# RWKV-7 head pairs in two merged instruction streams, dense products dealt out by a virtual clock

## The chip, the cores and the metric

One core of one Trainium2 chip runs the whole program. The metric is the device time of one execution in microseconds (us), the median of repeated runs; lower is better.

## The reference

Two layers, 512 tokens of width 1024, float32. Each layer adds half a SwiGLU feed-forward block, then a mixer of three branches, then a second half block. What matters here is the mixer, and in it the RWKV-7 branch with eight heads of 64:

```python
h = rms_norm(x, norm_mix[l])
proj = h @ w_in                                  # retention, sparse attention, rwkv and gate columns
y_ret, y_dsa = retention(...), sparse_attention(...)
# rwkv: token shift, low-rank decay and rate, normalised key kk, then for each token
def step(S, inp):
    r_t, w_t, k_t, v_t, kk_t, a_t = inp
    sa = jnp.einsum('bhvk,bhk->bhv', S, -kk_t)
    S = S * w_t[:, :, None, :] + sa[..., None] * (kk_t * a_t)[:, :, None, :] + v_t[..., None] * k_t[:, :, None, :]
    return S, jnp.einsum('bhvk,bhk->bhv', S, r_t)
# group norm of y over each head, + bonus, * g
merged = g_ret * (y_ret @ p_ret) + g_dsa * (y_dsa @ p_dsa) + g_rwkv * (y_rwkv @ p_rwkv)
x = x + merged @ w_out
```

## The kernel before

**Dense products.** Each float32 operand is split in a high and a low part (`split`, lines 49 and 50: ACT copies, DVE subtracts), and a product of 128x128 by 128x512 is three one-pass matmuls (`mm3`, lines 109, 111 and 113) into a PSUM bank with the tag psd (four banks). "A product" below is one of these three matmuls. Weights come through SP's queue into four raw buffers and three split ones.

**RWKV.** The eight heads are worked in four pairs. A pair has these steps, named as in the prediction:
- the front (`front2`): decay (lines 346-360, `cum`, `E`), rate, normalised key (line 373, the Newton steps `kkr` of `rsqrt`, `bc` in line 378 and its transposes by line 96), bonus (392, 393), and the stacked operands `bk` and `stk` (403 to 406), partly on DVE and partly on POOL;
- the mixing products z (line 421, four groups), with their two masked evacuations on DVE (426, 427);
- the inverse (in `mid`): the 32x32 diagonal blocks go through DRAM (`dn`) into N, one block a partition; POOL solves the triangular systems in 31 steps (466, 468); after every fourth a one-column "pace" matmul (470) stands in PE's order; the result goes through DRAM (`dx`) into `mt`, and two rounds of small matmuls (487, 492) join the blocks;
- the chain (`chain`): eight chunks of 64 tokens one after the other, each with four hops: A (line 504), copied to `cx`; B (514), copied to `uv`; C (524), which with `cb` gives the next state `sv`; and D (531), whose result goes to `Y`;
- the post (`post`): group norm of Y, transposes, bonus, gate (564), and y to DRAM.

The recurrence has two PSUM banks of its own (tag psr); retention and attention use two others (psf).

**Order.** A tile scheduler takes instructions by priority levels; `K.at("rec")` puts the recurrence in the first level. The other dense products of the mixer (retention, attention, gates, merge) are queued, and `K.fill(n, after=mm)` places n of them behind the matmul `mm`. How many stand behind which step was written in tables by hand: 11 behind each z group, 38 behind v's transposes, 12, 11, 11 or 15 behind each pace, 29 behind the last pace, 5 behind each join, 9, 7, 3 or 5 behind each hop of the chain, 46 behind the chain, and 6, 0, 2 or 7 that stand behind no step. Pairs follow one another: chain(p), the front, z and inverse of p + 1, then post(p). Retention and the index part of the attention run beside pairs 0 and 1, the attention's heads beside pairs 2 and 3, and the merge, which needs all three branches, comes last.

## Time and profile before

| what | value |
|---|---|
| median of 3 runs | 3111.48 us (3107.99 to 3112.62) |
| span of the profiled execution, first to last instruction | 3103.6 us |
| PE busy | 2990.3 us (96%) |
| DVE, ACT, POOL busy | 1761.8, 1081.5, 715.2 us |
| mean granted clock of PE | 0.975 |
| core, state | one core, clock as granted by the throttle |

The execution's own time is its span and some 8 us around it, by the median of the runs. PE is busy nearly throughout; matmuls are pipelined, so a busy PE is not PE at its peak, and at a granted clock of 0.5 the same work is busy twice as long. What an idle or slow stretch costs is read from windows of the span.

### The profile page before, as it was taken

To read this page: it belongs to the slowest core of one execution; us is meant where nothing else is said; L and a number is where in the kernel's file an instruction comes from. 1 tells how busy PE (TensorE), PEld (TensorE's weight loads), DVE (VectorE), ACT (ScalarE), POOL (GpSimd) and SP (SyncE) were. 2 spreads that over 40 slices of the span, in tenths; PEclk is the share of its full clock that TensorE was granted. 3 is DMA by queue.
4 is the path that set the end of the run, shared out by engine and by line. 5 is a ranking of instruction groups with operands and counts; after the bars stand their busy time and mean duration, and the time that the engine had idled before them with its cause. 6 is when DMAs were issued, how large, how long until landed. Compare 5 with 4: busy or idle time off the path is not lost.

```text
span 3103.6 us, 40717 instructions
## 1 busy us (share of the span) xinstructions
PE 2990.3 (96%) x14336; PEld 2373.5 (76%) x14336; DVE 1761.8 (57%) x3641; ACT 1081.5 (35%) x1892; POOL 715.2 (23%) x1186
## 2 busy tenths in 40 slices
PE   9999999999899999999999999999999899999998
PEld 7888877767667778888888888677776677788886
DVE  5443388758675675443344433887585746644433
ACT  4333343334333233333333333433333333333322
POOL 2110024342433031111011101243423340311100
PEclk9999999999899999999999999899999999999999
DMA  4223422223223452233322234222333135523232
GB/s 136 98 97 106 117 72 70 73 85 124 81 85 96 139 190 95 95 99 94 97 95 97 98 109 118 66 72 71 96 110 92 64 110 155 175 92 99 96 95 89
DMA packets 203580, 314.08 MB, mean 101 GB/s; under 512 B 46320, under 2 KB 60400, under 8 KB 203376
## 3 DMA queue, kind: packets, MB, share of 16 engines
q1 hardware_dynamic: 203376, 311.49, 32.2%
q8 instruction: 112, 1.84, 0.2%
q14 instruction: 92, 0.75, 0.1%
HBM read 277.86 MB, written 33.55 MB: 100 GB/s over the span
## 4 chain that ended last, share of the span: by engine, by line
PE 74%; DVE 10%; POOL 6%; DMA 6%; issue 3%; ACT 1%; SPq 0%; DVEq 0%; POOLq 0%; ACTq 0%
PE psd L113 22%; PE psd L109 22%; PE psd L111 22%; DMA N<-dn 3%; POOL cum L468 2%; POOL E L466 2%; DVE wlo L50 2%; PE psr L421 1%; DMA th<-th 1%; PE psr L504 1%; PE psf L96 1%; DMA dx<-cum 1%; DMA y<-y 1%; DVE cb L523 1%; PE psr L514 1%
## 5 line engine op out<-in xcount | busy, mean ns | idle before, releaser
L49 ACT ACTIVATE whi<-raw 128x512 fp32r<-128x512 f32 (+2 forms) x920 | 571.5, 622 | 1259.6 <-PE psd L111 927.2
L50 DVE TENSOR_TENSOR wlo<-raw,whi 128x512 fp32r<-128x512 f32 (+2 forms) x920 | 657.6, 715 | 560.0 <-ACT whi L49 543.9
L111 PE MATMUL psd<-xl,whi 128*128 128x512 f32 x2144 | 856.0, 399 | 2.4 <-DVE xl L161 2.4
L109 PE MATMUL psd<-xh,whi 128*128 128x512 f32 x2144 | 850.6, 397 | 1.5 <-DVE g L203 1.5
L113 PE MATMUL psd<-xh,wlo 128*128 128x512 f32 x2144 | 849.9, 396 | 0.1
L111 PEld LDWEIGHTS psd<-xl,whi 128*128 128x128 f32 x2144 | 406.7, 190 | 88.9 <-DVE xl L161 4.4
L109 PEld LDWEIGHTS psd<-xh,whi 128*128 128x128 f32 x2144 | 406.6, 190 | 88.5 <-issue 3.4
L113 PEld LDWEIGHTS psd<-xh,wlo 128*128 128x128 f32 x2144 | 406.9, 190 | 84.1 <-issue 1.4
L207 POOL TENSOR_TENSOR u<-s,u 128x512 f32<-128x512 f32 x88 | 141.2, 1605 | 841.0 <-DVE u L206 726.3
L109 PE MATMUL psd<-ah,whi 128*128 128x512 f32 x704 | 277.4, 394 | 0.0
L113 PE MATMUL psd<-ah,wlo 128*128 128x512 f32 x704 | 276.0, 392 | 0.0
L111 PE MATMUL psd<-al,whi 128*128 128x512 f32 x704 | 273.2, 388 | 0.0
L172 POOL TENSOR_TENSOR sq<-sq,sq 128x512 f32<-128x512 f32 x42 | 56.1, 1336 | 467.4 <-ACT sq L170 467.4
L113 PE MATMUL psd<-whi,xl 128*128 128x512 f32 (+1 forms) x384 | 160.6, 418 | 0.0
L111 PE MATMUL psd<-wlo,xh 128*128 128x512 f32 (+1 forms) x384 | 156.1, 407 | 0.0
L113 PEld LDWEIGHTS psd<-ah,wlo 128*128 128x128 f32 x704 | 132.1, 188 | 31.0
L109 PE MATMUL psd<-whi,xh 128*128 128x512 f32 (+1 forms) x384 | 155.1, 413 | 0.0
L111 PEld LDWEIGHTS psd<-al,whi 128*128 128x128 f32 x704 | 132.2, 188 | 29.6
L109 PEld LDWEIGHTS psd<-ah,whi 128*128 128x128 f32 x704 | 132.3, 188 | 26.3
L50 DVE TENSOR_TENSOR al<-u,ah 128x512 fp32r<-128x512 f32 x88 | 61.8, 702 | 153.6 <-ACT ah L49 153.4
L206 DVE TENSOR_TENSOR u<-psd,rb 128x512 f32<-128x512 f32 x88 | 60.9, 692 | 127.3 <-PE psd L113 127.3
L810 POOL TENSOR_SCALAR L<-L,mx 128x128 f32<-128x128 f32 (+3 forms) x64 | 71.4, 1118 | 199.4 <-DVE mx L809 99.0
(262 smaller groups left out, 3907.2 us busy)
## 6 DMA issues: line engine op xcount, KB each, us to landing
raw<-in_wf_dram SPq DMA_DIRECT2D x184, 256.0 KB
raw<-in_ffa_in_dram SPq DMA_DIRECT2D x176, 256.0 KB
raw<-in_ffb_in_dram SPq DMA_DIRECT2D x176, 256.0 KB
th<-th SPq DMA_DIRECT2D x96, 256.0 KB
raw<-in_ffa_out_dram SPq DMA_DIRECT2D x80, 256.0 KB
raw<-in_wt_dram SPq DMA_DIRECT2D x80, 256.0 KB
raw<-in_ffb_out_dram SPq DMA_DIRECT2D x80, 256.0 KB
x<-x SPq DMA_DIRECT2D x32, 256.0 KB
```

The costliest lines, as they stand in the source:

```text
L49: self.nc.scalar.activation(hi, x, AF.Copy)
L50: self.nc.vector.tensor_tensor(out=lo, in0=x, in1=hi.bitcast(F32), op=ALU.subtract)
L96: return self.nc.tensor.transpose(out, x, self.ident)
L109: nc.tensor.matmul(out, ah, bh, start=start, stop=False)
L111: nc.tensor.matmul(out, ah, bl, start=False, stop=False)
L113: nc.tensor.matmul(out, al, bh, start=False, stop=stop)
L172: nc.gpsimd.tensor_tensor(out=sq, in0=sq, in1=self.ssq[0], op=ALU.add)
L206: nc.vector.tensor_tensor(out=u, in0=pu, in1=self.rb, op=ALU.mult)
L207: nc.gpsimd.tensor_tensor(out=u, in0=s, in1=u, op=ALU.mult) # 2 * silu(g) * u
L466: nc.gpsimd.tensor_tensor(out=tv, in0=X[:, 0:n, u:u + 1].to_broadcast([P, n, w]), in1=N[:, u:u + 1, u + 1:].to_broadcast([P, n, w]), op=AL ...
L468: nc.gpsimd.tensor_tensor(out=X[:, 0:n, u + 1:], in0=X[:, 0:n, u + 1:], in1=tv, op=ALU.add)
L810: nc.gpsimd.tensor_scalar(out=x, in0=x, scalar1=mx[:, 3:4], scalar2=None, op0=ALU.mult)
```

## The change

The content of each engine is the same: the same matmuls, evacuations and transfers. What changes is the order, and the buffers that it needs.

- The front, z and inverse of a pair (`ahead`) and the chain and post of a pair (`behind`) become two generators that yield, after each step, a duration written by hand (in units of a microsecond: 4, 2, 4, 4, 5 for the front, 3 for each z group, 25 for the way to N, 4 for each pace, 15 for the way back, 2 for each join and each hop, 8 and 2 for the post).
- Two virtual clocks add up these durations. The stream whose clock is behind is traced next: so pair p + 1 is traced beside pair p. The chain of a pair starts when its `ahead` has ended.
- Each advance of the lower clock makes 3.2 products due for a unit; they are placed behind the last matmul traced (`self.mm`). The tables by hand go.
- `gch`, both `stk`, `zb`, `bkt`, both `sv` and `mt` get two buffers; to make room, N lies in a buffer of the tag `bk`, post uses one new tag `yq` in place of `rsq` and `bc`, two temporaries of retention and attention share other tags, and the scratch of the descriptors is set to 1024.
- The pace matmuls take a psr bank each time in place of one for all eight.

```diff
     def pairs(self, blk):
...
-        nxt = self.next(0)
-        for p in range(4):
-            d = nxt
-            K.fill(FM[p])
-            with K.at("rec"):
-                self.chain(d)
-            K.fill()
-            if p < 3:
-                nxt = self.next(p + 1)
-            with K.at("rec"):
-                self.post(d)
+        d, t, n, due = [None] * 4, [0.0, 0.0], [0, 0], 0.0
+        g = [self.ahead(d, p) for p in range(4)], [self.behind(d, p) for p in range(4)]
+        now = lambda: t[0] if n[1] == n[0] else t[1] if n[0] == 4 else min(t)
+        while n[1] < 4:
+            e = 0 if n[0] < 4 and (n[1] == n[0] or t[0] <= t[1]) else 1
+            was = now()
+            try:
+                with K.at("rec"):
+                    t[e] += next(g[e][n[e]])
+            except StopIteration:
+                n[e] += 1
+                if e == 0 and n[1] == n[0] - 1:
+                    t[1] = max(t)
+            else:
+                due += RATE * max(now() - was, 0.0)
+                if due >= 1:
+                    K.fill(int(due), self.mm)
+                    due -= int(due)
         self.done = True
...
+    def ahead(self, d, p):
+        self.K.fill()
+        d[p] = yield from self.front2(p, *self.rkv)
+        yield from self.mid(d[p])
+
+    def behind(self, d, p):
+        yield from self.chain(d[p])
+        yield from self.post(d[p])
...
-            if FI and (u % 4 == 3 or u == 30):
-                pace = nc.tensor.matmul(pz[0:1, u:u + 1], X[:, 0, u + 1:u + 2], K.ident[:, 0:1], start=True, stop=True)
-                K.fill(FI if u < 30 else FD, pace)
+            if u % 4 == 3 or u == 30:
+                self.mm = nc.tensor.matmul(K.ps("r")[0:1, 0:1], X[:, 0, u + 1:u + 2], K.ident[:, 0:1], start=True, stop=True)
+                yield 4 if u < 30 else 15
...
-            K.fill(FC[d["p"]], mm)
+            yield 2
```

In PE's program order, this is the front of pair 2 before, in the first layer, from the transposes of `bc` (line 96) to the first z group (421); names are out<-in, psr is the recurrence, psf the attention, psd the dense products:

```order
L96 MATMUL psr_7617<-ident,bc_7615 128x128 x4
L392 MATMUL psr_7626<-P_7627,bones_3109 128x512
L823 MATMUL psf_6061<-X_6067,v_3127 128x256
L393 MATMUL psr_7626<-P_7628,bones_3109 128x512
L824 MATMUL psf_6061<-X_6068,v_3127 128x256
L823 MATMUL psf_6061<-X_6067,v_3127 128x256
L824 MATMUL psf_6061<-X_6068,v_3127 128x256
L710 MATMUL psf_6082<-kh_3322,qs_5996 128x256
L711 MATMUL psf_6082<-kl_3323,qs_5996 128x256
L710 MATMUL psf_6091<-kh_3322,qs_5999 128x256
L711 MATMUL psf_6091<-kl_3323,qs_5999 128x256
L421 MATMUL psr_7648<-stk_1754_7636,bk_7638 128x128 x4
```

And this is PE's order after the change around the first z group of pair 1, in the first layer; lines have moved by 11 to 13: 515 is A, 525 B, 542 D of pair 0's chain, and 433 is pair 1's z:

```order
L515 MATMUL psr_5289<-sv_995_4238,stk_930_3960 128x64
L542 MATMUL psr_5219<-uv_1210_5251,zb_3993 64x64
L542 MATMUL psr_5219<-uv_1211_5252,zb_3993 64x64
L515 MATMUL psr_5289<-sv_996_4239,stk_931_3961 128x64
L111 MATMUL psd_5119<-wlo_5280,xh_2537 128x512
L113 MATMUL psd_5119<-whi_5279,xl_2538 128x512
L109 MATMUL psd_5120<-whi_5279,xh_2537 128x512
L433 MATMUL psr_5296<-stk_1206_5238,bk_5240 128x128 x4
L111 MATMUL psd_5120<-wlo_5280,xh_2537 128x512
L113 MATMUL psd_5120<-whi_5279,xl_2538 128x512
L109 MATMUL psd_5121<-whi_5279,xh_2537 128x512
L525 MATMUL psr_5289<-cx_5304,mt_4827 64x64 x2
```

A z group that had attention matmuls ahead of it and no dense product now stands inside a chain chunk of the pair before, with three products ahead of it and three behind.

On DVE, this is the stretch between the copies cx and uv of a chunk of pair 0's chain before (507 and 518), beside retention (601, 602, and the `rr` steps) and a split (50):

```order
L507 COPY cx_5204<-psr_5046 128x128
L601 TENSOR_TENSOR X_5053<-X_5053,rcc 128x256
L149 TENSOR_TENSOR rr_4783<-rr_4782 128x8
L602 TENSOR_TENSOR X_5053<-X_5053,m_5055 128x256
L150 SCALAR_TENSOR_TENSOR rr_4783<-rr_4783,ss_4754 128x8
L151 SCALAR_TENSOR_TENSOR rr_4782<-rr_4783,rr_4782 128x8
L50 TENSOR_TENSOR wlo_5256<-raw_5253,whi_5255 128x512
L518 COPY uv_1188_5206<-psr_5046 64x64
L518 COPY uv_1189_5207<-psr_5046 64x64
```

And the same stretch after, of the chunk shown above (518 is cx and 529 uv; 614 and 615 are retention's 601 and 602, 438 and 439 are the evacuations of pair 1's z):

```order
L518 COPY cx_5304<-psr_5289 128x128
L150 SCALAR_TENSOR_TENSOR rr_4518<-rr_4518,ss_4489 128x8
L614 TENSOR_TENSOR X_4998<-X_4998,rcc 128x256
L151 SCALAR_TENSOR_TENSOR rr_4517<-rr_4518,rr_4517 128x8
L615 TENSOR_TENSOR X_4998<-X_4998,S_5000 128x256
L149 TENSOR_TENSOR rr_4518<-rr_4517 128x8
L438 TENSOR_TENSOR zb_5295<-psr_5296,zmask 64x512
L439 TENSOR_TENSOR stk_1206_5238<-psr_5296,zmask 64x512
L150 SCALAR_TENSOR_TENSOR rr_4518<-rr_4518,ss_4489 128x8
L529 COPY uv_1220_5306<-psr_5289 64x64
L529 COPY uv_1221_5307<-psr_5289 64x64
```

Two evacuations of the other pair's z have come between the copies, where one split stood.

At the end of the first layer's RWKV work, PE's order before runs from the chain's last chunks (504 A, 514 B, 524 C, 531 D) to the first product of the merge (psd<-yh):

```order
L504 MATMUL psr_9504<-sv_1992_8819,stk_1966_8692 128x64
L531 MATMUL psr_9459<-uv_2130_9475,zb_8703 64x64
L531 MATMUL psr_9459<-uv_2131_9476,zb_8703 64x64
L504 MATMUL psr_9504<-sv_1993_8820,stk_1967_8693 128x64
L514 MATMUL psr_9504<-cx_9523,mt_9219 64x64 x2
L524 MATMUL psr_9504<-uv_2141_9525,bkt_8806 64x64
L524 MATMUL psr_9504<-uv_2142_9526,bkt_8806 64x64
L504 MATMUL psr_9560<-sv_1992_8819,stk_1966_8692 128x64
L531 MATMUL psr_9504<-uv_2141_9525,zb_8703 64x64
L531 MATMUL psr_9504<-uv_2142_9526,zb_8703 64x64
L504 MATMUL psr_9560<-sv_1993_8820,stk_1967_8693 128x64
L109 MATMUL psd_9431<-yh_2096_9383,whi_9434 128x512
```

After the change, the stretch ahead of the first product of the merge holds transposes of the attention and of Y (line 96), the attention's last matmuls (836, 837) and the gate (577); D of the last chunk stands ten rows further up, with no dense product in between:

```order
L96 MATMUL psf_6827<-ident,L_6794 128x128
L96 MATMUL psf_6827<-ident,L_6793 128x128
L96 MATMUL psf_6827<-ident,L_6794 128x128
L96 MATMUL psr_9731<-ident,Y_9158 64x128 x4
L96 MATMUL psr_9755<-ident,Y_9158 64x128 x4
L836 MATMUL psf_6813<-X_6832,v_3127 128x256
L837 MATMUL psf_6813<-X_6833,v_3127 128x256
L836 MATMUL psf_6813<-X_6832,v_3127 128x256
L837 MATMUL psf_6813<-X_6833,v_3127 128x256
L577 MATMUL psr_9770<-sg_3592,g_703_3107 128x512
L109 MATMUL psd_9614<-yh_2155_9566,whi_9617 128x512
L109 MATMUL psd_9695<-yh_2155_9566,whi_9698 128x512
```

The chain's last steps stood around the merge's first products; now the whole post stands ahead of them.

## Rows read from the trace of the kernel before

**Rows 1.** The page's busy times over the span: us, share, instructions.
```profile
PE 2990.3 (96%) x14336; PEld 2373.5 (76%) x14336; DVE 1761.8 (57%) x3641; ACT 1081.5 (35%) x1892; POOL 715.2 (23%) x1186
```

**Rows 2.** Busy time by stretches of the span, core 0: stretch, width, then busy us and instructions of PE, PE's weight loads, DVE, ACT, POOL, then PE's granted clock, the DMA share and GB/s. The second and fourth stretch of the program are the mixers; the one between them is the feed-forward block behind the first mixer and the one ahead of the second.
```profile
380.00:1170.00 790.00, 743.17 (x3842) 565.90 (x3842) 544.93 (x1291) 288.20 (x532) 261.91 (x523) 0.95 0.33 102
1170.00:1920.00 750.00, 750.00 (x3330) 620.39 (x3329) 331.45 (x524) 251.05 (x411) 91.52 (x65) 1.00 0.32 98
1920.00:2710.00 790.00, 742.03 (x3827) 564.60 (x3827) 545.04 (x1288) 287.23 (x531) 261.86 (x523) 0.95 0.33 102
```

**Rows 3.** The same columns, for the steps of the first layer's mixer: fronts with z, inverses with their transfers, pair 0's chain, and the passage to the merge.
```profile
422.00:454.00 32.00, 28.26 (x106) 20.33 (x106) 30.92 (x69) 8.45 (x17) 7.64 (x9) 0.79 0.15 46
454.00:506.00 52.00, 46.79 (x216) 34.26 (x215) 40.46 (x100) 19.23 (x33) 30.52 (x81) 0.97 0.24 72
506.00:612.00 106.00, 105.95 (x646) 80.84 (x645) 83.46 (x216) 35.47 (x61) 27.94 (x51) 1.00 0.24 76
612.00:648.00 36.00, 32.91 (x163) 25.67 (x163) 28.81 (x67) 12.02 (x22) 12.38 (x20) 0.92 0.23 70
648.00:702.00 54.00, 48.90 (x245) 36.93 (x244) 23.90 (x49) 20.30 (x38) 29.80 (x86) 0.97 0.30 90
...
766.00:812.00 46.00, 39.99 (x178) 30.36 (x178) 38.58 (x92) 15.87 (x33) 12.58 (x14) 0.85 0.24 74
812.00:864.00 52.00, 47.89 (x249) 36.29 (x248) 24.28 (x50) 21.51 (x41) 25.68 (x71) 0.97 0.33 98
...
912.00:956.00 44.00, 36.59 (x156) 26.98 (x155) 36.35 (x82) 13.58 (x26) 13.16 (x9) 0.84 0.20 62
956.00:1005.00 49.00, 45.65 (x227) 34.73 (x226) 19.42 (x38) 18.80 (x36) 25.37 (x69) 0.97 0.41 116
1018.00:1046.00 28.00, 25.37 (x140) 19.19 (x138) 16.31 (x49) 8.96 (x16) 1.51 (x6) 0.82 0.42 134
```

**Rows 4.** PE's waits over the span: what waited, for which line; us in total, times, longest.
```profile
PE psr L470 <- POOL cum L468: 25.4, 14, 4.9
PE psr L96 <- DVE bc L378: 19.7, 6, 4.4
...
PE psr L421 <- DVE bk L403: 7.8, 6, 2.7
```

**Rows 5.** The chain that ended last, pair 1 of the first layer, from the last z group to `mt`: start, us, what. The first row covers one z group (four matmuls, two records each).
```profile
640.00 1.10 PE psr L421 x8
...
642.20 1.62 DMA dn<-zb
643.91 10.71 DMA N<-dn
...
688.72 4.71 DMA dx<-cum
693.49 1.70 DMA mt<-dx
```

**Rows 6.** POOL's instructions of the inverse, over the span (eight inverses): count, busy us, mean ns, and the idle time ahead of them with what ended it.
```profile
L468 POOL TENSOR_TENSOR cum<-cum,E 128x60 f32<-128x60 f32 (+24 forms) x248 | 87.4, 353 | 16.9
L466 POOL TENSOR_TENSOR E<-cum,N 128x60 f32<-128x60 f32 (+24 forms) x248 | 80.2, 324 | 84.0 <-DMA N<-dn 59.9 <-issue 7.8
```

**Rows 7.** PE's timeline at the end of the first layer's RWKV work: start, us, instruction; in brackets the idle time ahead of it. 824 is the attention's last matmul, 514 and 524 are B and C of a chain chunk, psd<-yh the merge's first product.
```profile
1030.36 0.28 PE L824 MATMUL psf<-X,v 128*128 128x256 f32 x1
...
1033.37 0.48 PE L514 MATMUL psr<-cx,mt 64*64 64x64 f32 x4 [0.38 <-DVE cx L507]
1034.51 0.48 PE L524 MATMUL psr<-uv,bkt 128*64 128x64 f32 x4 [0.65 <-DVE uv L518]
...
1036.84 1.20 PE L109 MATMUL psd<-yh,whi 128*128 128x512 f32 x2
```

**Rows 8.** DVE's instructions by line over the span, those of the chain, of z's evacuations, of retention and of the splits: count, busy us, mean ns, idle time ahead.
```profile
L50 DVE TENSOR_TENSOR wlo<-raw,whi 128x512 fp32r<-128x512 f32 (+2 forms) x920 | 657.6, 715 | 560.0 <-ACT whi L49 543.9 <-DMA raw<-in_wf_dram 5.9 <-PE psd L113 5.3
...
L523 DVE TENSOR_SCALAR cb<-sv,gch 64x64 f32<-64x64 f32 x112 | 35.4, 316 | 2.1
L527 DVE SCALAR_TENSOR_TENSOR sv<-psr,gch,cb 64x64 f32<-64x64 f32 x112 | 31.6, 282 | 13.3 <-PE psr L524 10.7
...
L535 DVE TENSOR_TENSOR Y<-psr,cx 64x64 f32<-64x64 f32 x128 | 28.4, 222 | 9.9 <-PE psr L531 7.7
L518 DVE COPY uv<-psr 64x64 f32<-64x64 f32 x128 | 28.2, 220 | 25.5 <-PE psr L514 24.0 <-issue 0.2
...
L427 DVE TENSOR_TENSOR stk<-psr,zmask 64x512 f32<-64x512 f32 x32 | 22.0, 689 | 0.7
L426 DVE TENSOR_TENSOR zb<-psr,zmask 64x512 f32<-64x512 f32 x32 | 22.0, 687 | 9.9 <-PE psr L421 9.8
...
L601 DVE TENSOR_TENSOR X<-X,rcc 128x256 f32<-128x256 f32 x32 | 16.7, 522 | 13.5 <-POOL m L598 13.4
...
L602 DVE TENSOR_TENSOR X<-X,m 128x256 f32<-128x256 f32 x32 | 15.3, 479 | 0.2
```

**Rows 9.** DVE's second Newton operation on 128x8 elements, in the front (kkr) and in the retention (rr); the columns are those of the group above.
```profile
L150 DVE SCALAR_TENSOR_TENSOR kkr<-kkr,s 128x8 f32<-128x8 f32 x24 | 8.1, 337 | 0.5
...
L150 DVE SCALAR_TENSOR_TENSOR rr<-rr,ss 128x8 f32<-128x8 f32 x24 | 4.7, 194 | 0.3
```

More of the change, by code (lines that the diff above doesn't have):

```diff
@@ L275, in wide @@
         nc.tensor.matmul(z, self.wa[h][:, ch], self.lh[h], start=True, stop=False)
-        nc.tensor.matmul(z, self.wa[h][s, ch], self.ll[s], start=False, stop=True)
+        self.mm = nc.tensor.matmul(z, self.wa[h][s, ch], self.ll[s], start=False, stop=True)
         return z
@@ L314, in pairs @@
         K = self.K
-        K.run(self.lora(blk))
-        K.run(self.front(0, blk))
+        with K.at("norm"):
+            K.run(self.lora(blk))
+            K.run(self.front(0, blk))
         self.blk = blk
-        nxt = self.next(0)
-        for p in range(4):
-            d = nxt
-            K.fill(FM[p])
-            with K.at("rec"):
-                self.chain(d)
-            K.fill()
-            if p < 3:
-                nxt = self.next(p + 1)
-            with K.at("rec"):
-                self.post(d)
-        self.done = True
-    def next(self, p):
-        with self.K.at("rec"), ExitStack() as es:
-            if self.gate:
-                es.enter_context(self.tc.issue_after(self.gate.ins))
-            d = self.front2(p, *self.rkv)
-            self.mid(d)
-            return d
+        d, t, n, due = [None] * 4, [0.0, 0.0], [0, 0], 0.0
[16 more added lines that the diff above has]
+                    due -= int(due)
+        self.done = True
+    def ahead(self, d, p):
[5 more added lines that the diff above has]
+        yield from self.post(d[p])
     def front2(self, p, r, k, v):
@@ L372, in front2 @@
         for i in range(4):
-            nc.tensor.matmul(pss[:, 2 * i:2 * i + 2], sq[:, i * P:(i + 1) * P], c["ind2"], start=True, stop=True)
+            self.mm = nc.tensor.matmul(pss[:, 2 * i:2 * i + 2], sq[:, i * P:(i + 1) * P], c["ind2"], start=True, stop=True)
         s8 = self.t("s8", [P, 8])
@@ L392, in front2 @@
         nc.tensor.matmul(psb, self.bones, bh, start=True, stop=False)
-        nc.tensor.matmul(psb, self.bones, bl, start=False, stop=True)
+        self.mm = nc.tensor.matmul(psb, self.bones, bl, start=False, stop=True)
+        yield 4
         bv = self.t("bv", bufs=2)
@@ L420, in mid @@
                     ck = 4 * q + i
[L421 to L422 removed]
+                    self.mm = zl = nc.tensor.matmul(z[:, i * P:(i + 1) * P], bk[s, ck, :], st[h][s, ck, :], start=True, stop=True)
+                yield 3
                 z3 = z.rearrange("p (i t) -> p i t", i=4)
@@ L503, in chain @@
             for h in range(2):
-                mm = nc.tensor.matmul(a[:, 64 * h:64 * h + 64], st[h][:, ck, :], sv[h][:, ck, :], start=True, stop=True)
-            K.fill(FC[d["p"]], mm)
+                self.mm = nc.tensor.matmul(a[:, 64 * h:64 * h + 64], st[h][:, ck, :], sv[h][:, ck, :], start=True, stop=True)
+            yield 2
             X = self.t("cx", [P, P], bufs=2)
@@ L513, in chain @@
                 s = slice(64 * h, 64 * h + 64)
-                mm = nc.tensor.matmul(a[s, 256:320], mt[s, ck, :], X[s, s], start=True, stop=True)
-            K.fill(FC[d["p"]], mm)
+                self.mm = nc.tensor.matmul(a[s, 256:320], mt[s, ck, :], X[s, s], start=True, stop=True)
+            yield 2
             for h in range(2):
@@ L554, in post @@
             for ck in range(4):
-                last = K.turn(pt[0:64, ck * P:ck * P + P], Y[:, 4 * q + ck, :])
+                self.mm = last = K.turn(pt[0:64, ck * P:ck * P + P], Y[:, 4 * q + ck, :])
             for h in range(2):
```

59 lines of the change are left out of this document (29 added, 30 removed).

## The prediction

> **What bounds the kernel now.** I first read the page's busy shares: the TensorE (PE) works 2990.3 of 3103.6 us, the VectorE (DVE) 1762, GpSimd (POOL) 715 [rows 1]. So the whole is PE's, and a new order of the same instructions can give back only the time in which PE stands still or runs slow. Five stretches of the span, cut at the ends of the stages, say where that is [rows 2]: the feed-forward blocks are full (750.00 of 750.00 us between the two mixers, clock 1.00), the two mixers are not. The mixer of the first layer has 46.8 us of idle PE and a granted clock of 0.95, the second 48.0 us and 0.95. A product costs 750/3330 = 0.225 us in the full stretch, which is the unit of cover below.
>
> Next I cut the first mixer at the steps of its four pairs [rows 3]. What a stretch of w us loses to the clock is w x (1 - clock), since the records know two levels, 2.4 and 1.2 GHz, and half the speed for t us is t/2 lost. The reader is to see three kinds of stretch:
> - The fronts (422-454, 612-648, 766-812, 912-956): idle 3.74 + 3.09 + 6.01 + 7.41 = 20.3 us, clock 6.7 + 2.9 + 6.9 + 7.0 = 23.5 us. Together 43.8.
> - The inverses with their transfers (454-506, 648-702, 812-864, 956-1005): idle 5.21 + 5.10 + 4.11 + 3.35 = 17.8, clock 1.6 + 1.6 + 1.6 + 1.5 = 6.3. Together 24.1.
> - The chain of pair 0 (506-612) loses 0.05 us: it is covered by products already. The passage to the merge (1018-1046) loses 2.6 + 5.0.
>
> The waits confirm who is late [rows 4]: the pace product waits for POOL's inverse 25.4 us, the transposes of the key norm for DVE's bc 19.7 us, the z products for bk 7.8 us. In a front PE has hardly a product of its own and waits for a string of DVE and POOL steps; the stop also drops the granted clock behind it (0.79 in 422-454, 0.84 in 912-956), so a front costs twice what its idle says.
>
> **The change, part by part.** No instruction is added or removed that counts in this sum; products and steps change places, and buffers are doubled so that they can.
>
> Fronts. Those of pairs 1 to 3 now stand between the chain steps of the pair before them. The first piece of the order shows both: before, from the transposes of bc to z there is no dense product; now three stand ahead of z and three behind it, with the chain's matmuls around them. What is late there is then hidden by the chain's own cover, 18 to 20 products a chunk, some 4.3 us. I take the idle and the clock loss of these three fronts as gone: 16.5 + 16.8 = 33.3 us a mixer. Pair 0 has no chain to stand in. It gets more products (52, 38 and 28 ahead of its three waits, by the order, where it had 40, 15 and 0); of its 3.74 + 6.7 I leave 6. So 43.8 - 6 = 37.8 us a mixer.
>
> Inverses. Their length is POOL's and the queues': from the last z product (ended 641.1) N lands at 643.91 + 10.71 = 654.6, some 14 us later; the way back is 4.71 + 1.70 = 6.4 us [rows 5]. POOL's own work in one inverse is (87.4 + 80.2)/8 = 21 us [rows 6], and other POOL work stands among it. Nothing of that gets shorter. What changes is the cover: for pairs 1 to 3 the last chain chunks and the post of the pair before now lie in it, with about as many dense products as before (127, 143 and 124 from v's transposes to the joins, where there were 131, 142 and 133). I price that added work at 6 us or more each, against losses of 6.7, 5.7 and 4.8: these go but for 1 us each. Pair 0 gets none of it, and fewer products: 126 in the first layer and 93 in the second, where it had 142 and 144, partly made up by other matmuls. I leave its 6.8 us as it is. Left over 10, gained 14 us a mixer.
>
> Passage to the merge. All dense products that were kept for the merge are now dealt behind it: the last chain chunk, the attention's last products, Y's transposes and the first merge product stand without a dense product between them (last piece of the order). A bare hop of the chain is 1.1 us (1033.37 to 1034.51), and from the attention's last product to the first product of the merge it took 1036.84 - 1030.36 = 6.5 us [rows 7]. In before chain steps ran in this gap; now they lie ahead of it, three hops of 1.1 us bare and then the 6.5 us idle. That is 3.3 + 6.5 = 9.8 us more; I take 10 a mixer. From below it is 0, if the loads of the first y land earlier; from above 15, if the clock falls for longer than the 5.0 us of now.
>
> VectorE. In the overlapped chunks DVE has the chain's operations and the front's. The second piece of the order stands in a chunk of pair 0 that also holds two of pair 1's four z. Its DVE work [rows 8]: cx 0.28, two each of uv, sv, cb and Y 2.1, two pairs of z evacuations 2 x (0.69 + 0.69) = 2.8, the retention's two L601 and two L602 2.0, one split 0.7, seven small ones of some 0.2 each 1.4: 9.2 us. PE has in it 19 products, 4.3 us, two groups of z at 1.1 [rows 5] and 1 us of chain: 7.5. So PE waits 1.7 us. Adding such excesses over all chunks, priced in the same way, I get 33 us for the new order and 16 for the old one, both layers together: 17 us more. Bounds: 0, if the excess of one chunk is taken up in the next, and 35, if none is and PE's clock falls with it.
>
> The sum against the profiled span: 2 x (37.8 + 14) = 104 gained, 2 x 10 + 17 = 37 lost, 67 us less: 3103.6 - 67 = 3036.6. The median of the runs is 7.9 above that span, which lies around it and stays: 3111.5 - 67 = 3044 us.
>
> A rule against this. In the front, the same three-operation Newton step on 128x8 takes 0.34 us (kkr), and in the retention 0.19 (rr) [rows 9]: something holds DVE there, and in the front POOL works on 512-column operands. The Trainium skill, SBUF — State Buffer, section Who interferes with whom, says that a DVE instruction with two SBUF inputs contends with a GpSimd instruction that reads SBUF, and that the loser blocks fully. By that rule the trace agrees in direction; the chain's own operations take one input from PSUM or have only one in SBUF, and would be spared.
>
> **The rivals.**
> 1. Only the passage is paid for. All idle time and clock loss of fronts and inverses goes, DVE takes up its excess: 2 x 67.9 - 20 = 116, so 2995 us. For it: the chain of pair 0 lost 0.05 us in 106. Against it: pair 0's front and inverse have no second stream beside them.
> 2. POOL is held in the overlap. The front's POOL operations and the inverse run beside a fuller DVE (in 648-702 it was busy 23.9 of 54 us), and the front reaches z later. A front has six POOL operations on its string (lines 367, 391 and twice 404 and 406); held by one two-input DVE operation of 0.69 us each, the string gets 6 x 0.69 = 4.1 us longer, and PE waits that much longer at z. Six fronts make 25 us, so 3069. For it: the slow small steps of [rows 9]; against it: the same POOL operations stood beside a busy DVE before (30.92 of 32 us in 422-454). What the Trainium skill states in the section named above would work in this direction.
> 3. The fronts' gain does not come. DVE's string is as long as before and the chain now also stands in it, PE waits at bc and z with three products of cover, and the clock falls as before: of the 66.6 us of the six fronts nearly all stays, 3044 + 60 = 3104. For it: long waits of now are on that string [rows 4]; against it: 18 to 20 products a chunk.
> 4. Slower: every hop of the chain waits for one long DVE operation of the other stream, since DVE works in order. 8 chunks x 3 hops x 3 pairs x 2 layers = 144 hops at 0.69 us (one z evacuation) are 99 us; against the 84 that the rest of the sum gains (67 + 17) that is 15 slower, 3126 us. It decides from 84/144 = 0.58 us a hop. For it: a hop has three to seven products, 0.7 to 1.6 us, and a bare one already takes 1.1; against it: a front has only four z and about ten other long operations, not one for every hop.
>
> **How the numbers follow.** My forecast has 0.44, with a range of its own of 3015 to 3070 from the bounds of the passage (0 to 15 a mixer) and of DVE (0 to 35). Rival 1 has 0.18, rival 2 0.10, rival 3 0.14, rival 4 0.14. A difference under 0.2%, 6 us, can't be told from none here. Rival 3 lies about that bound, half of it counts as same. Faster 0.44 + 0.18 + 0.10 + 0.07 = 0.79, same 0.07, slower 0.14. The range goes from rival 1 to just past rival 3: 2992 to 3110; outside stay rival 4 and a few hundredths of rivals 1 and 3.
>
> **What would show it.** In the profile after, the two mixers' stretches should be some 33 us shorter each, with PE's clock in them at 0.97 or more; the waits for bc should fall from 19.7 to under 6 us, and those for bk should be small; the wait for POOL's inverse should stay at about half, nearly all in pair 0. New should be waits for cx, uv and sv of some 10 to 20 us in all, and an idle stretch ahead of the first merge product in each layer. I am wrong if the chain's waits exceed 50 us, or if the pace or z of pairs 1 to 3 still waits as it did.

## The result, and the profile after

The changed kernel takes 3130.6 us (median; 3127.8 to 3134.7), where the kernel before takes 3112.1 in the same comparison: ratio 1.0062, 95% interval 1.0047 to 1.0076. It is 0.6% slower; the forecast was 3044 us and faster, with a range of 2992 to 3110. The span, the page's busy times and three stretches of the span, in the columns of [rows 1] and [rows 2]:

```profile
span 3131.3 us, 40635 instructions
...
PE 3000.4 (96%) x14336; PEld 2377.3 (76%) x14336; DVE 1746.7 (56%) x3641; ACT 1082.1 (35%) x1892; POOL 724.5 (23%) x1186
```

```profile
380.00:1170.00 790.00, 732.85 (x3770) 555.61 (x3769) 529.42 (x1279) 279.92 (x520) 262.63 (x520) 0.94 0.32 98
1170.00:1920.00 750.00, 750.00 (x3319) 619.62 (x3318) 335.34 (x526) 254.39 (x416) 94.47 (x64) 1.00 0.33 101
1920.00:2710.00 790.00, 735.94 (x3800) 558.44 (x3799) 525.18 (x1277) 279.70 (x518) 261.97 (x523) 0.95 0.32 98
```

PE's work has not changed (14336 instructions); the feed-forward blocks are full as before. The span is 27.7 us longer where the medians differ by 18.5: the time of an execution is some 2 us above its span (here 3133.05 and 3131.3), not the 8 taken before, so the profiled execution of the kernel before was some 6 us quicker than its median. Both mixers have more idle time and the same or a lower clock. PE's waits over the span, of the kind of [rows 4] (823 is the attention's scaling on POOL, before line 810; 481 the pace, before 470; 515, 525, 535 are A, B, C of the chain; 577 the gate):

```profile
PE psf L96 <- POOL L L823: 23.4, 10, 6.2
PE psr L481 <- POOL cum L479: 11.6, 11, 2.4
PE psr L515 <- DVE bv L406: 10.3, 4, 3.8
...
PE psd L109 <- ACT yh L49: 9.4, 4, 4.4
...
PE psr L96 <- DVE Y L560: 5.2, 2, 2.6
...
PE psr L535 <- DVE uv L529: 4.4, 3, 3.3
...
PE psr L525 <- DVE cx L518: 3.7, 3, 1.3
PE psr L433 <- DVE Y L546: 3.1, 3, 1.9
```

The wait for bc (19.7 us before) and that for bk (7.8) are gone from the head of this list, the pace waits 11.6 us in place of 25.4, and the chain's cx and uv stay small, as forecast. The wait of the attention's transposes for POOL has grown (10.9 us before, 23.4 now); new are those of A for bv and of the merge's first product for its operand.

To see where it is lost, the first mixer is divided in both kernels at PE's own marks: start of the first front, first pace and first join of each pair, first merge product, first output product. So the windows are: front 0; inverse 0; chain 0 with front 1; inverse 1; chain 1 with front 2; inverse 2; chain 2 with front 3; inverse 3; chain 3 to the merge; merge. A window of a front ends at the first pace, so z and the way to N lie in it. Before:

```profile
412.80:473.00 60.20, 54.12 (x226) 39.89 (x224) 55.59 (x126) 22.04 (x43) 15.22 (x27) 0.89 0.21 66
473.00:509.00 36.00, 33.13 (x157) 23.99 (x157) 24.75 (x56) 13.02 (x21) 26.57 (x69) 0.95 0.21 60
509.00:658.00 149.00, 141.60 (x819) 108.43 (x818) 113.73 (x284) 49.42 (x86) 43.03 (x82) 0.98 0.24 75
658.00:695.70 37.70, 37.54 (x173) 28.44 (x173) 16.44 (x30) 15.45 (x25) 26.48 (x73) 0.95 0.27 83
695.70:826.30 130.60, 120.39 (x660) 91.78 (x660) 99.38 (x269) 49.56 (x108) 30.23 (x55) 0.95 0.34 109
826.30:858.70 32.40, 31.41 (x141) 23.30 (x141) 14.32 (x29) 12.41 (x23) 21.44 (x57) 0.95 0.25 74
858.70:969.00 110.30, 99.02 (x561) 73.26 (x560) 78.86 (x213) 39.60 (x81) 30.82 (x46) 0.94 0.27 85
969.00:999.50 30.50, 30.31 (x136) 22.40 (x136) 11.01 (x23) 10.74 (x20) 20.88 (x56) 0.94 0.30 87
999.50:1036.80 37.30, 34.05 (x231) 25.69 (x232) 22.63 (x61) 13.82 (x26) 5.67 (x8) 0.92 0.42 133
1036.80:1139.00 102.20, 100.57 (x468) 78.34 (x468) 70.11 (x134) 30.41 (x51) 25.21 (x23) 0.98 0.54 169
```

And after:

```profile
412.10:476.80 64.70, 64.16 (x298) 49.22 (x296) 56.25 (x120) 29.60 (x55) 20.59 (x40) 1.00 0.25 75
476.80:519.30 42.50, 37.63 (x164) 28.02 (x165) 30.41 (x77) 11.81 (x20) 23.39 (x64) 0.76 0.22 61
519.30:639.00 119.70, 113.73 (x647) 85.71 (x643) 93.38 (x235) 37.53 (x67) 38.24 (x79) 0.93 0.23 68
639.00:682.50 43.50, 39.98 (x213) 30.13 (x212) 27.76 (x68) 13.86 (x23) 26.55 (x58) 0.92 0.25 73
682.50:779.40 96.90, 90.97 (x526) 69.20 (x523) 70.61 (x191) 37.39 (x80) 29.86 (x58) 0.95 0.35 111
779.40:825.20 45.80, 35.56 (x168) 25.86 (x165) 26.14 (x69) 13.51 (x28) 25.75 (x65) 0.89 0.25 69
825.20:921.20 96.00, 91.29 (x532) 69.08 (x528) 63.45 (x174) 36.25 (x73) 22.79 (x34) 0.96 0.29 91
921.20:961.50 40.30, 34.67 (x165) 24.73 (x163) 20.62 (x55) 12.29 (x24) 24.40 (x62) 0.92 0.28 81
961.50:1059.60 98.10, 88.24 (x506) 65.55 (x503) 58.84 (x168) 34.65 (x65) 16.95 (x21) 0.97 0.31 96
1059.60:1157.20 97.60, 93.02 (x386) 71.82 (x385) 54.47 (x73) 30.12 (x50) 22.12 (x14) 0.98 0.60 179
```

Idle time is width less PE's busy time, the clock's loss is width x (1 - clock). Added for both layers (the second divided at the same marks), in us:

| window | before: idle + clock | after | difference |
|---|---|---|---|
| front 0 | 13.2 + 13.3 | 1.5 + 0.0 | -25.0 |
| chain 0, front 1 | 15.5 + 7.4 | 12.1 + 17.5 | +6.7 |
| chain 1, front 2 | 20.5 + 11.7 | 12.9 + 8.7 | -10.6 |
| chain 2, front 3 | 22.6 + 13.2 | 8.4 + 5.7 | -21.7 |
| inverse 0 | 5.6 + 5.2 | 10.6 + 20.3 | +20.1 |
| inverse 1 | 0.2 + 4.2 | 3.5 + 3.5 | +2.6 |
| inverse 2 | 1.9 + 3.2 | 18.4 + 12.0 | +25.3 |
| inverse 3 | 0.9 + 3.7 | 13.2 + 6.7 | +15.3 |
| chain 3 to merge | 6.4 + 6.0 | 19.7 + 5.9 | +13.2 |
| merge | 3.8 + 4.1 | 9.0 + 3.9 | +5.0 |
| sum | 163 | 193 | +31 |

The sum agrees with the 28 us of the span. It is of one profiled execution of each kernel, and runs of one kernel differ by up to 15 us, so a few us in one window carry no argument. The windows of the fronts give back 51 us; those of the inverses take 63, and the passage with the merge 18. In the program order the inverse windows hold 77, 94, 102 and 94 dense products in the first layer and 44, 99, 102 and 95 in the second; before it was 104, 113, 103, 99 and 106, 113, 103, 99. The last chain holds the products that the others lack: 229 and 228, where 74 and 73 stood.

A second division, near that of [rows 3], runs from the last z product of a pair to its first join, so that the way to N belongs to the inverse. Pair 2 of the first layer, before and after:

```profile
807.70:858.70 51.00, 46.89 (x216) 35.42 (x216) 22.31 (x48) 21.16 (x41) 25.95 (x71) 0.97 0.32 95
```

```profile
755.70:824.90 69.20, 57.52 (x282) 42.36 (x282) 43.76 (x124) 23.89 (x51) 32.41 (x84) 0.90 0.30 88
```

In this division the inverses of pairs 1 to 3 lose 35 us before and 79 after, both layers together, with 149 to 154 products in a window before and 145 to 153 after. Of their idle time (23 us before, 49 after) the pace's wait for POOL's inverse was 15.1 us and is 1.4: what the inverse itself held up is covered now. In its place PE waits for the strings that were laid beside it: 19.8 us for the attention's scaling, 12 for the chain and the post (Y and uv), 8 for retention, 6 for the attention's other steps.

Inside the window of inverse 2 two waits make 9.6 of its 10.2 us of idle time. PE's timeline there, then DVE's step that makes the factor of the scaling, and POOL's queue just ahead of the second wait's end:

```profile
788.16 0.33 PE L96 MATMUL psf<-ident,L 128*128 128x128 f32 x1 [3.37 <-POOL L L823]
...
801.41 0.48 PE L96 MATMUL psf<-ident,L 128*128 128x128 f32 x1 [6.24 <-POOL L L823]
```

```profile
796.10 0.15 DVE L822 RECIPROCAL mx<-mx 128x1 f32<-128x1 f32 x1
```

```profile
799.86 0.26 POOL L477 TENSOR_TENSOR E<-cum,bk 128x35 f32<-128x35 f32 x1
800.20 0.26 POOL L479 TENSOR_TENSOR cum<-cum,E 128x35 f32<-128x35 f32 x1
800.43 0.92 POOL L823 TENSOR_SCALAR L<-L,mx 128x256 f32<-128x256 f32 x1
```

The factor is ready at 796.25, but the scaling 823 that PE waits for stands behind steps of the inverse (477, 479) in POOL's queue and starts only at 800.43.

### The profile page after: what moved, and what is told of

Its sections match the earlier page's. It is cut to its first block, busy times and chain, and to the rows that moved or that the text cites. A ratio compares the mean times of both kernels' runs of the same rounds, so it can differ in the third digit from the quotient of the medians.

```text
span 3131.3 us, 40635 instructions
## 1 busy us (share of the span) xinstructions
PE 3000.4 (96%) x14336; PEld 2377.3 (76%) x14336; DVE 1746.7 (56%) x3641; ACT 1082.1 (35%) x1892; POOL 724.5 (23%) x1186
## 4 chain that ended last, share of the span: by engine, by line
PE 79%; DVE 8%; POOL 5%; DMA 4%; issue 3%; ACT 1%; SPq 0%; DVEq 0%; POOLq 0%; ACTq 0%
PE psd L109 23%; PE psd L113 23%; PE psd L111 23%; DVE wlo L50 2%; POOL cum L479 2%; POOL E L477 2%; DMA bk<-dn 1%; DMA th<-th 1%; PE psf L96 1%; PE psr L433 1%; PE psr L515 1%; PE psf L665 1%; DMA y<-yg 1%; PE psf L667 1%; PE psf L724 1%
## 5 line engine op out<-in xcount | busy, mean ns | idle before, releaser
L113 PE MATMUL psd<-whi,xl 128*128 128x512 f32 (+1 forms) x384 | 154.1, 402 | 0.0
L109 PE MATMUL psd<-whi,xh 128*128 128x512 f32 (+1 forms) x384 | 147.4, 405 | 0.0
```

Source lines behind the costliest of these rows:

```text
L109: nc.tensor.matmul(out, ah, bh, start=start, stop=False)
L113: nc.tensor.matmul(out, al, bh, start=False, stop=stop)
```

## The experiments

All are the kernel before or the changed one with the edit shown; the ratio is to runs of the kernel before on the same chip, with its 95% interval. "After" is 3131, "before" 3107 to 3112. Window sums are for both layers, as in the table.

**POOL's queue: the attention's scaling on ACT.**

```diff
-nc.gpsimd.tensor_scalar(out=x, in0=x, scalar1=mx[:, 3:4], scalar2=None, op0=ALU.mult)
+nc.scalar.activation(x, x, AF.Copy, scale=mx[:, 3:4])
```

In the changed kernel:

> The changed kernel with the attention's scaling of its weights (line 823, one operation a head and query tile, 64 in all) on ACT in place of POOL; nothing else. Theory 'POOL's queue': the attention waits behind the inverse's steps, which now stand beside it, so the wait of the transposes for line 823 (23.4 us in the changed kernel, 10.9 before) goes to under 5 us, idle falls by about 20 us and the clock loss behind these stops by some 10: about 3100 us. Theory 'two PSUM banks': the wait goes, but PE then waits for the recurrence at the next place; at most 10 us faster, about 3122.

Measured: 3117.7 us, ratio 1.0022 (1.0013 to 1.0031), 13 us faster than after, between what the two theories said. The wait for 823 is 2.8 us, but this stands at the head of the list now:

```profile
PE psr L577 <- DVE yq L571: 19.2, 3, 6.7
```

The windows of inverses 2 and 3, where the wait was, lose 33 and 24 us, where after loses 30 and 20. The gate's product, which waits for the post's last evacuations on DVE (yq), has taken its place. So in the inverses POOL's queue is where PE waited, not why: with the wait gone, PE has no other work there either. The 13 us came from elsewhere, most from chain 3 to the merge (25.6 to 12.3): there the attention's last transposes, which waited for the scaling in the changed kernel, are through before the chain ends, so at this place POOL's queue did cost time.

In the kernel before:

> The kernel before with the same scaling on ACT. Its wait there is 10.9 us. Theory 'POOL's queue': 8 to 15 us faster than before, 3097 to 3104, which is what the move is worth without the merged streams; the difference of this run from the one above tells what the merged order itself costs. Theory 'two banks': the same.

Measured: 3123.4 us, 1.0034 (1.0022 to 1.0047): slower, which neither theory had. The list has more waiting for z (14.9 us in place of 7.8) and the pace (35.7 for 25.4), and less for bc (9.1 for 19.7). The scheduler places other instructions too when one moves; that this is what shifts a schedule fitted by hand by 13 us is the likely reading, not one that a run isolates.

**Two PSUM banks: the front's small products in psf.**

```diff
-pss = K.ps("r")   (and psi, psb)
+pss = K.ps()
```

> The changed kernel with the three small products of the front (squares for the key norm, transposes of bc, bonus) in the banks of retention and attention (psf) in place of the recurrence's two (psr). Theory 'two PSUM banks': the waits of chain step A for bv (10.3 us) and of z and the transposes for Y (5.6 us) shrink to under 5 in all, with the clock loss behind them some 20 us faster, about 3110. Theory 'POOL's queue': these waits only move to the next step of the same string, no more than 5 us faster, or slower, since the attention then waits for these banks.

Measured: 3445.1 us, 1.1074 (1.1059 to 1.1089), slower, as its second theory allowed, but by 314 us more than after. PE now waits most for the strings that share the two banks of retention and attention; the longest waits grew to:

```profile
PE psf L96 <- POOL L L823: 79.7, 56, 2.8
PE psf L96 <- DVE bc L388: 33.6, 8, 5.7
```

This says that putting the front's steps into that ring of two banks is dear, not what the recurrence's ring costs in the changed kernel. For that there is the next one.

**The bonus moved out of the front, behind v's transposes** (its lines 396 to 406 go there, unchanged):

> The changed kernel with the bonus (its split, two products and bv) moved out of the front, behind v's transposes, where the way to N is waited for. Theory 'two banks': chain step A no longer waits for the bank that the bonus holds until bv (10.3 us), and the front's z comes a step earlier: 10 to 20 us faster, 3110 to 3120. Theory 'DVE is full in the overlap': the wait moves to the next step, 3130 within 6.

Measured: 3128.1 us, 1.0065 (1.0053 to 1.0077). The wait of A for bv is gone from the list and the time stays within 3 us of 3131; the pace waits 17.2 us in place of 11.6, the transposes of Y 8.6 in place of 5.2, cx 8.0 in place of 3.7, and the scaling less (14.6 in place of 23.4). The wait that went was made up by others along the strings.

**Buffers: the kernel before with all buffers of the change, and with one.**

```diff
-N = self.t("N", [P, 32, 32])
+N = self.t("bk", [P, 8, P]).rearrange("p c t -> p (c t)").rearrange("p (s t) -> p s t", s=32)
```

> The kernel before, in its order by hand, with all buffers of the change (two each of gch, stk, zb, bkt, sv, mt; N in bk; yq; the shared tags of retention and attention; the small descriptor scratch). If the order is what costs: 3112 within 6 us. If the shared buffers cost (retention's m in S, the attention's X of six): 3120 or more, and then part of the 19 us is theirs.

> The kernel before with one edit of the change alone: N, the inverse's operand, lies in the buffer of bk. N's load then waits for the last reader of bk, the transposes behind z, which end 5.5 us after the last z group; with all shared buffers the inverse's first step came 16.2 us behind it on the mean, in the kernel before 14.0. If this sharing is what the shared buffers cost: first step at 16 us or later, and 8 x 2.2 = 18 us slower, with the clock loss behind it 3122 to 3130. If another of the buffers costs, or only that the scheduler's order shifted: 3112 within 6 us.

Measured: all buffers 3127.2 us, 1.0054 (1.0041 to 1.0066); N in bk alone 3123.4, 1.0046 (1.0033 to 1.0059). So one line, on an edit that I had costed at nothing, carries most of what the buffers cost in the old order (14 of 17 us). PE's timeline in that kernel, pair 1: the last z group and the two transposes of bk; then the inverse's first step on POOL:

```profile
641.44 1.16 PE L421 MATMUL psr<-stk,bk 64*128 64x128 f32 x8
...
644.09 0.60 PE L96 MATMUL psr<-ident,bk 128*128 128x128 f32 x4
...
647.75 0.60 PE L96 MATMUL psr<-ident,bk 128*128 128x128 f32 x4
```

```profile
659.07 0.24 POOL L466 TENSOR_TENSOR E<-cum,bk 128x31 f32<-128x31 f32 x1 [7.89 <-DMA bk<-dn]
```

N's load waits for the second group of transposes (647.75); in the kernel before it had landed at 654.6 for a z group that started at 640.0 [rows 5]. Over the eight pairs the first step comes 16.1 us behind z in place of 14.0. What is lost is nearly all clock: idle time over the mixers' windows is 88 us (91 before), the clock's loss 102 us (72 before).

**bk's transposes ahead of z**, so that bk has no reader behind z (the block that makes `bt` is moved up by 20 lines). In the changed kernel, alone, and with the bonus moved and the scaling on ACT:

> The changed kernel with bk's transposes traced ahead of the z groups, so that N's load need not wait for them. In the changed kernel they end 8.1 us after the last z group and the inverse's first step comes at 18.4 us. Theory 'sharing N with bk': first step back at 14 to 15 us, the pace waits fall and the kernel gets 10 to 20 us faster, 3110 to 3120. Theory 'two banks' or 'POOL's queue': in the merged order PE reaches the joins late anyway (15 us behind the inverse's end, where the way back takes 7), so the inverse has slack, and the time stays at 3130 within 6.

> The changed kernel with all three: bk's transposes ahead of z, the bonus behind v, and the attention's scaling on ACT (3118 alone). If their causes are apart and add up: 13 + 10 + 10 or more faster than 3131, below 3100 and so faster than the kernel before. If one loss only takes the place of another: 3110 to 3118.

Measured: 3089.9 us, 0.9939 (0.9928 to 0.9951), 41 us faster than after and faster than before; all three together 3095.5, 0.9953 (0.9941 to 0.9965). The inverse's first step comes 13.2 us behind z in place of 18.4. But PE reached the joins 15 us behind the inverse's end in after, and 19 here, so the inverse had slack, and the gain, twice the most that was expected, is spread: over the window table front 1 -6, front 2 -5, inverse 0 -5, inverse 3 -11, passage -13. The controls in the old order:

> The kernel before with N in the buffer of bk, as in b_N (3123), but with bk's transposes traced ahead of the z groups, so that bk has no reader left behind z. If b_N lost because N's load waits for these transposes: the inverse's first step comes at 14 us or earlier again and the time is 3110 within 6 us. If it lost because the order shifted: still 3118 or more.

> The kernel before, N in its own buffer, with bk's transposes ahead of the z groups: the control for what that move is worth by itself in the old order. If the move only frees bk for N: 3110 within 6 us. If it helps by itself (the inverse's stretch has fewer steps, z starts later): more than 6 us off, and that part of the 41 us by which the changed kernel gained from it is not due to the sharing.

Measured: N in bk 3127.1 us, 1.0059 (1.0045 to 1.0073); N in its own buffer 3131.1, 1.0075 (1.0061 to 1.0088). The move costs 22 us by itself in the old order (its fronts are bare, and two more steps stand ahead of z: a reason, not a test), and then sharing costs nothing more. So the 2 us of delay in the inverse's start are shown; that they make the 14 us of b_N is not.

**How many products stand beside the two streams: RATE** in place of 3.2:

> The changed kernel with RATE 2.6 in place of 3.2: 1269 products are dealt out beside the recurrence in place of 1562, the rest comes behind it. Theory 'cover is short in the overlap': fewer products a hop, more waits for cx, uv, sv and the pace, 15 to 30 us slower, 3145 to 3160. Theory 'what waits is a bank, POOL's queue or a transfer': the end of the recurrence comes earlier and the merge later, within 8 us of 3131.

> The changed kernel with RATE 3.8: 1854 products due. Theory 'cover is short': waits in the overlap get fewer, 10 to 20 us faster, 3110 to 3120, if the products last to the end. Theory 'bank, queue or transfer': within 8 us of 3131, or slower, since the products run out before the last chain.

> The changed kernel with RATE 3.4. If the time follows the cover smoothly: between 3131 and 3102, about 3120. If the order's accidents are as large as its trend: more than 10 us off that line.

Measured: 2.6: 3203.2 us (1.0301, 1.0285 to 1.0316), far more than the 15 to 30 us expected; 3.4: 3107.3 (1.0000, 0.9991 to 1.0009); 3.8: 3102.2 (0.9980, 0.9969 to 0.9990). The cover is short: over the whole range the time follows it. The window of chain 0 with front 1 has 167, 258 and 348 products in the first layer at 2.6, 3.2 and 3.8, and both layers' windows lose 67, 30 and 9 us. Between neighbours it does not hold: at 3.4 there are 283 and the windows lose 32, and the three of chain and front 71 where they lose 65 at 3.2, though the kernel is 23 us faster, 13 off what its expectation gave for a smooth line. So the gain from 3.2 to 3.4 is not the fronts' cover. Of 3.8, the three windows of chain and front, and the last chain:

```profile
522.20:659.10 136.90, 135.55 (x810) 105.50 (x810) 106.86 (x262) 49.38 (x87) 53.04 (x105) 1.00 0.26 77
...
697.90:801.80 103.90, 102.56 (x595) 78.41 (x594) 78.72 (x214) 41.73 (x90) 28.12 (x48) 1.00 0.37 114
...
849.80:954.50 104.70, 103.67 (x601) 79.07 (x601) 69.06 (x177) 41.52 (x82) 25.28 (x38) 1.00 0.34 102
...
1001.10:1035.80 34.70, 28.18 (x193) 20.27 (x190) 19.42 (x69) 8.09 (x18) 6.02 (x13) 0.56 0.14 42
```

The reader sees the overlap as it was forecast (1.35, 1.34 and 1.03 us of idle time, clock 1.00), and what paid for it: the last chain, with one product left, at a granted clock of 0.56.

**Where the products stand.** The rate while both streams run, and the rate for the last chain and post:

```diff
-due += RATE * max(now() - was, 0.0)
+due += (3.45 if n[0] < 4 else 1.45) * max(now() - was, 0.0)
```

> The changed kernel with 3.45 products a unit while both streams run and 1.45 for the last chain and post, in place of 3.2 throughout: 428 x 3.45 + 60 x 1.45 = 1564 products, as many as before this edit (1562). Theory 'cover is short in the overlap, the place counts': the overlapped fronts lose a third to a half of what they lose at 3.2, 10 to 20 us faster than 3131, 3111 to 3121. Theory 'the number counts' (what is gained at 3.8 is gained at the end, since the attention gets done earlier): 3131 within 6, or slower.

> The changed kernel with the pace step's virtual duration 6 in place of 4, and 3.2 products a unit while both streams run, 1.2 for the last chain (1621 in all). The inverse windows of pairs 1 to 3 get 104 to 115 products where the changed kernel has 94 to 102, the fronts 265 to 336 where it has 228 to 291. Theory 'want of products in the inverse windows': they lose 20 us less over both layers, the fronts 25 less, below 3100. Theory 'the strings of post and attention beside the inverse are what waits': the inverse windows keep their 60 us, and only the fronts gain, 3100 to 3115.

Measured: a_two 3095.5 us, 0.9961 (0.9948 to 0.9974), 35 us faster than after with as many products, more than its theory said. a_pace_two (3.2 and 1.2, and a pace of 6) 3088.1, 0.9948 (0.9937 to 0.9960), the fastest here, and 0.5% faster than before. In it the windows of inverses 1 to 3 lose 44 us (57 after), those of chain and front 29 (65 after); inverse 0, whose 77 and 44 products did not change, loses 31 as it did. The 13 us of inverses 1 to 3 can't be put down to the ten products more in each: in a_two, with 99, 101 and 95 products there, these windows lose 40. Whether products there help stays open: at rates of 2.6, 3.2 and 3.8 the inverses of pairs 1 to 3 lose 41, 57 and 67 us from the first pace, and 91, 79 and 69 from the last z. What holds throughout is the order: from the last z to the first join they lose 62 to 91 us in all thirteen kernels of the merged order (a_fbank, with its other banks, left aside), with 128 to 227 products in a window, and 35 to 47 in the six of the old order, with 134 to 164.

**Both together.** bk's transposes ahead of z, with rates of 3.5, 3.8, and of 3.6 and 1.8:

> The changed kernel with bk's transposes ahead of z (3090 at 3.2) and RATE 3.5. If the two gains are apart: half of the 29 us that 3.8 gave, 3070 to 3080. If they remove the same loss: 3085 to 3095.

> The same with RATE 3.8. If apart: 3090 - 29 = 3061, up to 3070. If they remove the same loss: 3085 to 3100, the last chain being bare as without the transposes' move.

> The changed kernel with bk's transposes ahead of z, 3.6 products a unit while both streams run and 1.8 for the last chain and post (1649 in all). If cover in the overlap and an end with products are both wanted and both gains are apart: 3060 to 3075, the fastest of all. If the end needs no products, as the merge's lie beside it: not better than 3.8 throughout.

Measured: 3120.9 us (1.0041, 1.0029 to 1.0053), 3103.3 (0.9985, 0.9977 to 0.9994) and 3096.0 (0.9956, 0.9944 to 0.9969), all slower than expected. The gains do not add up. With the transposes ahead the time is 3090, 3121 and 3103 at 3.2, 3.5 and 3.8, without them 3131, 3107 (at 3.4) and 3102. The 41 us that the move gave at 3.2 are nothing at 3.8, and between the two the kernel with the move is 14 us slower: they belong to that one schedule, not to the earlier inverse.

## Why the prediction was wrong, step by step

**Fronts.** Forecast: 75.6 us less in both layers, with 17 of DVE's excess set against it, net 58.6. The four windows that hold the fronts, and the chains with them, gave 51. Near in sum by luck, as the parts show: front 0 gave 25, where I left it 12 of loss and it kept 1.5 (207 products in its window where 137 stood); front 1 gave nothing. There the step that failed is "the chain's own cover, 18 to 20 products a chunk". Before, chain 0 had 27 a chunk for itself and front 1 had products of its own, 350 in the window; merged, the two share 258. The streams were laid beside each other, and their cover was not added, it shrank by a quarter; RATE 3.8 gives it back, and the window's loss falls from 30 to 9.

**Inverses.** This is the step by which the prediction failed. Forecast: 28 us less ("these go but for 1 us each", pair 0 as it is). Measured: 63 more, 91 off, which turns 67 less into 24 more (60 more in the second division, which is nearer to that of the forecast). I had taken the last chain chunks and the post as cover, because they are PE work. They are work with waits of its own: Y for its normalisation, the gate for yq, and beside them the attention's heads, whose scaling stood behind the inverse on POOL. The wait for POOL's inverse did go, as forecast; these came in its place, and the loss of pairs 1 to 3 rose from 35 to 79 us in the second division, with nearly the same products. It is 62 or more in all thirteen kernels of the merged order and 47 or less in the six of the old one, whatever the number of products: the loss goes with the merged order, and 46 of its 49 us of idle time in the changed kernel are waits of the strings beside the inverse. Taking one of their waits away (a_act) left the windows' loss as it was, so no single one of them is shown to be the cause. For pair 0 I had counted that its products fall (in the window from the first pace, from 104 to 77 and from 106 to 44), and yet left its loss "as it is": it tripled, from 11 to 31 us, 20 of that by the clock. The last four paces of the first layer have no product between them, and retention's matmuls stand there; that this is the reason was not tested.

**Passage.** Forecast 20 us more, measured 18, 5 of them behind the merge's first product. Of the 9.8 us of its sum most are seen, though not as it was made up: in the first layer the merge's first product waits 4.34 us at 1059.3, where 6.5 were taken, and ahead of it the chain's last two hops leave PE idle 1.9 us and the attention's tail with the gate 3.5, partly for POOL's scaling, which the sum had not.

**DVE.** The waits for cx, uv and sv came to some 10 us in all, the low end of the 10 to 20 that I had written; what I had not seen is that the streams share the two banks of the recurrence (A for bv 10.3 us, z for Y 3.1). a_bonus takes the first of these away and gains nothing clear: a place where PE waits, not a cause.

**Buffers.** I costed them at nothing. N in bk delays the inverse by 2.1 us in the old order; in the merged order the inverse is through 15 us before PE reaches the joins, so this delay is within its slack.

**The base and the signs.** That 7.9 us lie around the span is wrong, as said above; it moves the forecast by nothing, since the 67 us were taken from the median. Its own range does not follow from its bounds: 20 and 17 us less, or 10 and 18 more, give 3007 to 3072, not 3015 to 3070. Of the signs, those for the waits came: bc fell from 19.7 to under 1 us, the pace to 11.6, 10 of them in pair 0, and the chain's waits stayed far under 50. The mixers, from first front to first output product, are 19 and 10 us longer in place of 33 shorter, at a clock of 0.94 and 0.95. Neither sign of being wrong showed, because neither looked at the strings that were new beside the inverse.

**Rival 2** (POOL held by a fuller DVE) did not come. One of the front's POOL operations that it priced, before and after (line 404 is 415 now), then POOL's inverse operations and DVE's Newton step in the front, over the span after, in the columns of [rows 6] and [rows 9]:

```profile
L404 POOL TENSOR_TENSOR bk<-kh,cum 64x512 f32<-64x512 f32 x16 | 20.7, 1291 | 1.0
```

```profile
L415 POOL TENSOR_TENSOR bk<-kh,cum 64x512 f32<-64x512 f32 x16 | 21.2, 1322 | 1.0
```

```profile
L479 POOL TENSOR_TENSOR cum<-cum,E 128x60 f32<-128x60 f32 (+24 forms) x248 | 85.8, 346 | 17.0
L477 POOL TENSOR_TENSOR E<-cum,bk 128x60 f32<-128x60 f32 (+24 forms) x248 | 83.4, 336 | 84.6 <-DMA bk<-dn 53.4 <-issue 14.0
```

```profile
L150 DVE SCALAR_TENSOR_TENSOR kkr<-kkr,s 128x8 f32<-128x8 f32 x24 | 6.6, 276 | 0.3
```

The operations of the front take 1291 and 1322 ns, 1324 and 1282, 1506 and 1484, 1407 and 1467 (404, 406, 367 and 391, before and after): none is longer by the 690 ns of the rival's price. A pair of inverse operations takes 682 ns on the mean, before it took 677; kkr fell from 337 to 276 ns. The Trainium skill, SBUF — State Buffer, section Who interferes with whom, has DVE operations with two SBUF inputs contend with POOL's reads of SBUF; the slow kkr of before agrees with it in direction, but no lengthening by the overlap is seen here.

Rival 3 (the fronts' gain does not come, 3104) and rival 4 (hops wait for DVE, 3126) were nearest in time, but neither is what happened: the fronts' gain came, all but that of front 1, and the hops wait some 10 us in all where rival 4 took 99. What I lacked was a rival by which the inverse's windows get worse.

What stays open: how much of a difference of 10 to 30 us between two neighbouring settings is the schedule's accident. The old order loses 13 to 22 us from edits that should be neutral (b_act, b_bk), and the merged one, with bk's transposes ahead of z, gets 31 us slower from 3.2 to 3.5 and 18 faster from there to 3.8. That the changed kernel is 0.6% slower than before, and five of its neighbours 0.4 to 0.6% faster, is in part the accident of one schedule; that its inverses lose more is not.

## What to carry to other kernels

When two strings of latency-bound steps are laid beside each other under a third kind of work that fills their gaps, count the filler for each window after the merge, not for each string before it: here the first two merged windows had three quarters of the products that the same strings had one after the other, and those of the inverses 7% fewer. Do not count work with waits of its own as cover: beside the inverse it brought more waits than it hid. And where a scheduler sets the order, run neighbours of a setting before crediting a gain to its mechanism.

## What the runs showed of the hardware

In the two mixers the clock costs nearly as much as the stops themselves (72 us beside 91 of idle time before, 84 beside 109 after). I had expected it to follow the idle time, and it need not: in b_N the idle time fell by 3 us and the clock's loss rose by 30. Nor has a busy PE the full clock. In inverse 0 of the changed kernel there is a stretch in which PE is busy throughout, nearly all with retention's matmuls and with no product; it had stood idle on and off in the 15 us before:

```profile
499.80:509.30 9.50, 9.50 (x30) 6.82 (x28) 4.22 (x11) 3.61 (x6) 1.21 (x6) 0.50 0.23 41
```

Its granted clock is 0.50, the lower of the two levels. In the last chain at RATE 3.8, PE is busy 28.18 of 34.7 us by the records, with the small matmuls of chain and attention, at 0.56. The Trainium skill, TensorE: Matmul & The Clock Gate, section A second HAM failure mode: psum-queue depth-cycling, tells of a kernel in which short, frequent stops of PE cost throughput by clock changes though its matmuls at full clock are as fast as elsewhere. No run here shows that: PE has 77 stops of over 0.15 us in the mixers of b_N, and 76 before.
